# 64 tokens of block 2 gathered instead of 32 in a hybrid attention, mLSTM and PEER block

## The chip, the cores and the metric

The kernel runs on one core of one Trainium2 chip. The metric is the device time of one execution in microseconds; the number to compare is the median of several executions. The profile and its rows come from one further execution, with the hardware profiler on.

## The reference

One decoder layer over 512 tokens (and 16 meta tokens) of width 2048, all in float32. A mixer of differential attention and mLSTM comes first; its result is added to the residual stream. Then comes the part that this case is about, PEER, a layer of 16,384 small experts, of which each token takes 128:

```python
q = (ht @ w_q).reshape(T, PEER_HEADS, 2, PEER_SUB_DIM)
s = jnp.einsum('thpd,hpnd->thpn', q, sub_keys)
...
best_s, best_pos = lax.top_k(cand_s, PEER_TOPK)
idx = jnp.take_along_axis(cand_i, best_pos, axis=-1).reshape(T, PEER_HEADS * PEER_TOPK)
gate = jax.nn.softmax(best_s, axis=-1).reshape(T, PEER_HEADS * PEER_TOPK)
...
ub = jnp.take(u, ib, axis=0)
act = jax.nn.gelu(jnp.einsum('td,tkd->tk', hb, ub), approximate=False)
return jnp.einsum('tk,tkd->td', gb * act, jnp.take(v, ib, axis=0))
```

u and v are tables of 16,384 rows of 2048 floats (128 MB each). The residual is added and the result normalised.

## The kernel before

The tokens of PEER are four blocks of 128. The kernel treats them in two ways.

**Dense.** For the first ND = 352 tokens (blocks 0, 1 and 96 tokens of block 2) it computes all 16,384 experts. The table u is streamed in 128 chunks (`u_chunk`): a chunk of 128 experts is a 128 x 2048 slab, loaded in two halves of 512 KB from SP's queue, each split into a high and a low part (`split_half`: ACT casts hi, VectorE computes lo), and multiplied in 3 x 16 = 48 matmuls of ND columns (`mm3`, three products for float32 accuracy). ACT takes the gelu and stores the chunk of activations to `Ad`. The high and low parts have five buffers of half a chunk, the raw loads three.

Which expert a token takes is a one-hot matter: `ebuild` makes, for four tokens at a time, one-hot rows (`e`, `eg` on VectorE, `ea` on ACT, in bf16), `gbuild` multiplies them in 12 small matmuls (`pg`) into the gate matrix of these four tokens over all experts, and every 32 tokens (`TG`) a 2 MB store on SP's queue puts them in `Gd`. In the second half (V), the product of activation and gate is made per chunk (`p_mul` on VectorE, `p_split`: an ACT cast ah and a VectorE subtraction al) and the table v is streamed in 240 steps, each a half of 512 KB and 24 matmuls of ND columns (`tmm`, `py`), with `yadd` after each group, and a last group of 16 steps that transposes the result (`seed`, `vmm`).

**Gathered.** The other tokens, block 3 (128 tokens) and the last NB = 32 tokens of block 2, have their rows fetched. One gather step (`gather`, then `work`) is an indirect DMA from GpSimd that brings 128 rows of 8 KB, one for each partition, into one of three buffers `ug`, and one VectorE operation over 128 x 2048: a dot product with the token (rows of u, L844), or a weighted addition (rows of v, L857). Block 3 needs 128 steps for u and 128 for v. The NB tokens of block 2 are spread over the partitions in NQ = 128/NB groups of slots, so that they need SB = 128/NQ steps each way. `run(n)` carries the steps out up to the n-th of NJ and keeps three gathers ahead.

**Order.** PE's and VectorE's instructions are issued in the order written. In a chunk of U that is: the two VectorE splits of the next chunk, then the one-hots, then the gather steps that `pace` calls for; a gather is issued when the step three before it has left its buffer. `pace` spreads the steps up to the JU-th over the chunks from the first with one-hots to the end of U; V spreads the rest over its steps. The last UTAIL = 6 chunks of U stand in the V block, where they alternate with V's first preparations (`pro`).

Of the kernel before, what the change touches and what calls it, by code (L numbers as in the profile page):

```python
# [10 lines left out]
BF = mybir.dt.bfloat16  # L11
U32 = mybir.dt.uint32
I32 = mybir.dt.int32
AF = mybir.ActivationFunctionType
OP = mybir.AluOpType
# [14 lines left out]
NK = 128  # L30
# [5 lines left out]
UTAIL = 6  # L36
# [1 line left out]
VLL = 6  # L38
GLAG = 8
QPRE = 24  # L40
NB = 32
NQ = 128 // NB
SB = 128 // NQ
ND = S - 128 - NB
GROUPS = [8] + [16] * 7 + [8]
NJ = 2 * (128 + SB)
JU = 150
AR = 20
AR1 = 8

# [1 line left out]
def bcast(ap, n):  # L52
    return bass.AP(tensor=ap.tensor, offset=ap.offset, ap=[list(a) for a in ap.ap] + [[0, n]])


def bcast_mid(ap, n):
    a = [list(p) for p in ap.ap]
    return bass.AP(tensor=ap.tensor, offset=ap.offset, ap=a[:1] + [[0, n]] + a[1:])
# [607 lines left out]
def rest(tc, I, out, L):  # L666
    nc = tc.nc
# [18 lines left out]
    with tc.tile_pool(name="op", bufs=1) as op_, tc.tile_pool(name="pso", bufs=6, space=PSUM) as pso:  # L686
# [34 lines left out]
        for i, (p, pr) in enumerate(seq):  # L721
# [13 lines left out]
            for j in range(2):  # L735
                n = 2 * pr + j
# [6 lines left out]
            if p == 4 and pr in (2, 5):  # L743
                b = stores.pop(0)
# [41 lines left out]

    hB = dp.tile([NB, D], F, name="hB")
    hn = []
    for b in range(2):
        cs = slice(1024 * b, 1024 * b + 1024)  # L790
        t = wp.tile([128, 8, 128], F, name="nfr", tag="raw", bufs=3).rearrange("p a b -> p (a b)")
        src = I["nfr"][0:1, cs]
        nc.sync.dma_start(t, bass.AP(tensor=src.tensor, offset=src.offset, ap=[[0, 128], [1, 1024]]))
        t2 = wp.tile([128, 8, 128], F, name="hB", tag="raw", bufs=3).rearrange("p a b -> p (a b)")
        nc.vector.tensor_tensor(t2[128 - NB:], x1n[128 - NB:, 2, cs], t[128 - NB:], op=OP.mult)
        nc.scalar.dma_start(hB[:, cs], t2[128 - NB:])
        nc.vector.tensor_tensor(t, x1n[:, 3, cs], t, op=OP.mult)
# [19 lines left out]
    up = sU.enter_context(tc.tile_pool(name="up", bufs=1))  # L817
    iota = up.tile([128, 128], F, name="iota")
    nc.scalar.dma_start(iota, I["c_iota"])
    iota4 = up.tile([128, 128, 4], BF, name="iota4")  # L820
    nc.vector.tensor_copy(iota4, bcast(iota, 4))
    n1T = up.tile([128, ND], BF, name="n1T")
    n2T = up.tile([128, ND], BF, name="n2T")
    gp = up.tile([128, 3, ND], BF, name="gp")
    g0 = up.tile([128, ND], F, name="g0")
# [6 lines left out]
    def gather(j):  # L832
        kind, k = jobs[j]
        t = rows[j] = gr.tile([128, D], F, name="ug", tag="ug", bufs=3)
        ix = idx if kind in "da" else idxB
        nc.gpsimd.indirect_dma_start(out=t, out_offset=None, in_=I["un" if kind in "dD" else "vn"],  # L836
                                     in_offset=bass.IndirectOffsetOnAxis(ap=ix[:, k:k + 1], axis=0))
# [21 lines left out]
    def run(n, ready=NJ):  # L859
        while nj[1] < min(n, ready):  # L860
            while nj[0] < min(ready, nj[1] + 3):
                gather(nj[0])
                nj[0] += 1
            work(nj[1])
            nj[1] += 1
        while nj[0] < min(ready, nj[1] + 3):
            gather(nj[0])
            nj[0] += 1
# [23 lines left out]
    with tc.tile_pool(name="tk", bufs=1) as tk, \  # L892
# [142 lines left out]
        for q in range(NQ):  # L1035
            ps_, cs = slice(NB * q, NB * q + NB), slice(SB * q, SB * q + SB)
            nc.vector.tensor_copy(idxB[ps_], ids[128 - NB:, 2, cs])
# [8 lines left out]
        for src, dst in ((n1s, n1T), (n2s, n2T), (gs, None)):  # L1046
            pt = ptr.tile([128, ND], F, name="ptt", tag="ptt")
            for b in range(3):
                n = min(128, ND - 128 * b)
# [14 lines left out]
    with tc.tile_pool(name="gk", bufs=1, reuse_waits="tile") as gk, \  # L1064
            tc.tile_pool(name="psg", bufs=2, space=PSUM) as psg, \
            tc.manual_schedule(engines={mybir.EngineType.Pool}):
        stg = {}

        ge = {}

        def ebuild(q):
            t0 = 4 * q
            e = gk.tile([128, 2, 128, 4], BF, name="e", tag="e", bufs=2)
            eg = gk.tile([128, 2, 128, 4], BF, name="eg", tag="eg", bufs=2)
            ea = gk.tile([128, 4, 128], BF, name="ea", tag="ea", bufs=2)
            nc.vector.tensor_tensor(e[:, 0], iota4, bcast_mid(n1T[:, t0:t0 + 4], 128), op=OP.is_equal)
            nc.vector.tensor_tensor(e[:, 1], iota4, bcast_mid(n2T[:, t0:t0 + 4], 128), op=OP.is_equal)
            for i in range(2):
                nc.vector.tensor_tensor(eg[:, i], e[:, 1], bcast_mid(gp[:, 1 + i, t0:t0 + 4], 128), op=OP.mult)
            for j in range(4):  # L1080
                nc.scalar.activation(ea[:, j, :], e[:, 1, :, j], AF.Copy, scale=g0[:, t0 + j:t0 + j + 1])
            ge[q] = e[:, 0], [ea.rearrange("p j n -> p n j"), eg[:, 0], eg[:, 1]]

        def gbuild(q):
            tg, r = divmod(4 * q, TG)
            if r == 0:
                stg[tg] = gk.tile([128, NK, TG], F, name="stg", tag="stg")
            e1, eg = ge.pop(q)
            pg = psg.tile([128, 4, 128], F, name="pg", tag="pg")
            for j in range(4):  # L1090
                for i in range(3):
                    nc.tensor.matmul(pg[:, j, :], e1[:, :, j], eg[i][:, :, j], start=(i == 0), stop=(i == 2))  # L1092
            nc.scalar.copy(stg[tg][:, :, r:r + 4], pg.rearrange("p j n -> p n j"))
            if r + 4 == TG:
                nc.sync.dma_start(Gd[tg, :, 0:NK, :], stg[tg])

        gr2.append(sG.enter_context(tc.tile_pool(name="gr2", bufs=1, side="right")))
        acc["D"] = gr2[0].tile([128, D], F, name="h2nB", tag="h2nB")
        for q in range(NQ):
            nc.scalar.dma_start(acc["D"][NB * q:NB * q + NB], hB)  # L1100
        ng, n0, c0 = 0, nj[1], ci
        ebuild(0)

        def pace(c):
            run(n0 + int((c + 1 - c0) * (JU - n0) / (NK - c0)))

        for c in range(ci, NK - UTAIL):
            u_chunk(c)
            while ng < min(ND // 4, (c + 1 - ci) * (ND // 4) / (NK - 12 - ci)):
                gbuild(ng)  # L1110
                ng += 1
                if ng < ND // 4:
                    ebuild(ng)
            pace(c)
    sU.close()

    with ExitStack() as sV:
# [46 lines left out]
        def vsplit(i):  # L1164
            if i < len(vord):
                vs[i] = split_half(None, "v", vraw.pop(i))
# [6 lines left out]
        free, t0 = [], 0  # L1173
        for g in range(NG - 1):
            n = GROUPS[g]
            free += [t0 + n + 2 * (j // 2) + 2 for j in range(n)]
            t0 += 2 * n
        for q in range(GROUPS[0], NK):
            g = max(x for x in range(NG) if g0s[x] <= q)
            m, n = q - g0s[g], GROUPS[g - 1]  # L1180
            base = 2 * g0s[g - 1]
            t = base + (2 * n * m) // GROUPS[g]
            t = max(t, free[q - AR] if q >= AR else 0, base - 4)
# [9 lines left out]
        for c in range(NK - UTAIL, NK):  # L1193
            if c == NK - 1:
                for i in range(VLA):
                    vload(i)
                    vsplit(i)
            u_chunk(c)
            for _ in range(-(-len(pro) // (NK - c))):
                f, q = pro.pop(0)  # L1200
                f(q)
            pace(c)
        assert not pro
        sQ.close()
        sD.close()
# [111 lines left out]
        for i, (g, hf, pr, c) in enumerate(vord[:last]):  # L1317
# [9 lines left out]
            if i == nlast - 8:  # L1327
                for b in range(2):
                    t = wp.tile([128, 8, 128], F, name="nlw", tag="raw", bufs=3)
# [134 lines left out]
```

## Time and profile before

| what | before |
|---|---|
| median of 3 runs (lowest to highest) | 3327.83 us (3327.72 to 3330.03) |
| the profiled execution | 3331.74 us |
| its span, first to last instruction | 3330.0 us |
| mean granted TensorE clock | 0.992 of full speed |
| matmul busy (PE) | 3264.0 us, 98% |
| VectorE busy (DVE) | 2320.2 us, 70% |
| ScalarE busy (ACT) | 1325.5 us, 40% |
| GpSimd busy (POOL) | 943.9 us, 28% |
| moved by DMA | 815.47 MB, 245 GB/s over the span |

Busy times of one engine are unions of its instructions' spans; instructions of one engine may overlap slightly. PE is the matmul, PEld the weight load that goes beside it. The DMA share of a stretch is the time that packets took, over 16 DMA engines and the stretch. Lines (L844) are those of the kernel before.

### The profile page before, as it was taken

To read this page: it belongs to the slowest core of one execution; us is meant where nothing else is said; L and a number is where in the kernel's file an instruction comes from. 1 tells how busy PE (TensorE), PEld (TensorE's weight loads), DVE (VectorE), ACT (ScalarE), POOL (GpSimd) and SP (SyncE) were. 2 spreads that over 40 slices of the span, in tenths; PEclk is the share of its full clock that TensorE was granted. 3 is DMA by queue.
4 is the path that set the end of the run, shared out by engine and by line. 5 is a ranking of instruction groups with operands and counts; after the bars stand their busy time and mean duration, and the time that the engine had idled before them with its cause. 6 is when DMAs were issued, how large, how long until landed. Compare 5 with 4: busy or idle time off the path is not lost.

```text
span 3330.0 us, 51020 instructions
## 1 busy us (share of the span) xinstructions
PE 3264.0 (98%) x20126; PEld 3067.1 (92%) x20126; DVE 2320.2 (70%) x3504; ACT 1325.5 (40%) x2219; POOL 943.9 (28%) x942
## 2 busy tenths in 40 slices
PE   8999999999999999999999999997999999999998
PEld 7889898888887899999999999997999999999996
DVE  7444444444367788787877778767888888888973
ACT  5444444453252233444544544433333333333323
POOL 2011111110015566423332233322323323323312
PEclk8999999999999999999999999998999999999999
DMA  4222121123353266588888978999999999999972
GB/s 154 70 70 77 64 77 64 64 70 115 127 186 136 87 221 226 206 323 316 332 343 325 361 297 348 354 362 337 377 354 375 372 365 370 375 364 372 379 279 101
DMA packets 230162, 815.47 MB, mean 245 GB/s; under 512 B 21697, under 2 KB 85697, under 8 KB 186529
## 3 DMA queue, kind: packets, MB, share of 16 engines
q1 hardware_dynamic: 105488, 400.72, 33.3%
q0 software_dynamic: 46080, 335.56, 25.7%
q10 hardware_dynamic: 78352, 75.92, 6.8%
q8 instruction: 158, 2.59, 0.3%
q14 instruction: 84, 0.68, 0.1%
HBM read 757.33 MB, written 54.79 MB: 244 GB/s over the span
## 4 chain that ended last, share of the span: by engine, by line
PE 85%; DVE 8%; DMA 2%; issue 2%; ACT 1%; POOL 1%; ACTq 0%; SPq 0%; POOLq 0%; DVEq 0%
PE pu L89 10%; PE pu L90 10%; PE pu L91 10%; PE py L1275 8%; PE py L1277 8%; PE py L1276 8%; PE ps L89 5%; PE ps L91 5%; PE ps L90 5%; PE pg L1092 3%; PE po L742 2%; PE po L740 2%; PE po L741 2%; DVE y L857 1%; DVE lov L80 1%
## 5 line engine op out<-in xcount | busy, mean ns | idle before, releaser
L89 PE MATMUL pu<-hh,hid 128*128 128x352 f32 (+1 forms) x2272 | 759.8, 334 | 0.2 <-ACT at L889 0.2
L90 PE MATMUL pu<-hh,lod 128*128 128x352 f32 (+1 forms) x2272 | 751.3, 331 | 3.1 <-DVE lod L80 3.1
L91 PE MATMUL pu<-hl,hid 128*128 128x352 f32 (+1 forms) x2272 | 750.2, 330 | 0.0
L1275 PE MATMUL py<-ah,hiv 128*128 128x352 f32 x1920 | 627.0, 327 | 20.5 <-ACT hiv L79 9.5
L1276 PE MATMUL py<-ah,lov 128*128 128x352 f32 x1920 | 623.4, 325 | 8.8 <-DVE lov L80 8.8
L1277 PE MATMUL py<-al,hiv 128*128 128x352 f32 x1920 | 625.5, 326 | 0.0
L79 ACT CAST hiv<-rawv 128x1024 fp32r<-128x1024 f32 x256 | 269.2, 1053 | 572.4 <-PE py L1277 462.6
L80 DVE TENSOR_TENSOR lod<-rawd,hid 128x1024 fp32r<-128x1024 f32 x284 | 361.0, 1287 | 176.7 <-ACT hid L79 175.5
L90 PEld LDWEIGHTS pu<-hh,lod 128*128 128x128 f32 x2272 | 428.2, 188 | 12.8 <-DVE lod L80 3.4
L89 PEld LDWEIGHTS pu<-hh,hid 128*128 128x128 f32 x2272 | 429.9, 189 | 10.3 <-ACT at L889 0.8
L91 PEld LDWEIGHTS pu<-hl,hid 128*128 128x128 f32 x2272 | 428.1, 188 | 9.7
L79 ACT CAST hid<-rawd 128x1024 fp32r<-128x1024 f32 x284 | 297.8, 1050 | 347.2 <-DMA rawd<-in_u_dram 235.1
L89 PE MATMUL ps<-xh,hiz 128*128 128x256 f32 (+2 forms) x1280 | 410.9, 321 | 1.3 <-DVE qT L369 1.2
L836 POOL DMA_INDIRECT ug<-in_un_dram,idx x128 | 249.2, 1947 | 522.3 <-DVE ug L844 500.8
L91 PE MATMUL ps<-xl,hiz 128*128 128x256 f32 (+2 forms) x1280 | 392.8, 307 | 0.0
L90 PE MATMUL ps<-xh,loz 128*128 128x256 f32 (+2 forms) x1280 | 392.5, 307 | 0.0
L1275 PEld LDWEIGHTS py<-ah,hiv 128*128 128x128 f32 x1920 | 363.0, 189 | 24.2 <-issue 12.9
L1276 PEld LDWEIGHTS py<-ah,lov 128*128 128x128 f32 x1920 | 362.6, 189 | 11.8 <-DVE lov L80 11.8
L836 POOL DMA_INDIRECT ug<-in_vn_dram,idx x128 | 229.0, 1789 | 469.7 <-DVE y L857 444.3
L1277 PEld LDWEIGHTS py<-al,hiv 128*128 128x128 f32 x1920 | 361.9, 188 | 0.0
L80 DVE TENSOR_TENSOR lov<-rawv,hiv 128x1024 fp32r<-128x1024 f32 x256 | 313.4, 1237 | 33.7 <-ACT hiv L79 33.5
L857 DVE SCALAR_TENSOR_TENSOR y<-ug,act,y 128x2048 f32<-128x2048 f32 x127 | 298.3, 2349 | 14.8 <-DMA ug<-in_vn_dram,idx 14.8
(342 smaller groups left out, 5029.9 us busy)
## 6 DMA issues: line engine op xcount, KB each, us to landing
rawd<-in_u_dram SPq DMA_DIRECT2D x256, 512.0 KB
rawv<-in_v_dram SPq DMA_DIRECT2D x256, 512.0 KB
rawz<-in_wz_dram SPq DMA_DIRECT2D x98, 512.0 KB
Ad<-at ACTq DMA_DIRECT2D x128, 176.0 KB
Gd<-stg SPq DMA_DIRECT2D x11, 2048.0 KB
gt<-Gd ACTq DMA_DIRECT2D x32, 704.0 KB
av<-Ad ACTq DMA_DIRECT2D x64, 352.0 KB
rawwo<-in_wo_dram SPq DMA_DIRECT2D x40, 512.0 KB
```

The costliest lines, as they stand in the source:

```text
L79: nc.scalar.copy(hi, raw)
L80: eng.tensor_tensor(lo, raw, hi.bitcast(F), op=OP.subtract)
L89: nc.tensor.matmul(ps, a, xh[k][:, cs], start=(k == 0), stop=False)
L90: nc.tensor.matmul(ps, b, xh[k][:, cs], start=False, stop=False)
L91: nc.tensor.matmul(ps, a, xl[k][:, cs], start=False, stop=(k == KD - 1))
L740: nc.tensor.matmul(ps[tb], mh[n][:, sl], h, start=(n == 0), stop=False)
L836: nc.gpsimd.indirect_dma_start(out=t, out_offset=None, in_=I["un" if kind in "dD" else "vn"], in_offset=bass.IndirectOffsetOnAxis(ap=ix[:, ...
L857: nc.vector.scalar_tensor_tensor(acc[kind], t, o, acc[kind], op0=OP.mult, op1=OP.add)
L1092: nc.tensor.matmul(pg[:, j, :], e1[:, :, j], eg[i][:, :, j], start=(i == 0), stop=(i == 2))
L1275: nc.tensor.matmul(po, h, ah, start=(pr + j == 0), stop=False)
L1276: nc.tensor.matmul(po, l, ah, start=False, stop=False)
L1277: nc.tensor.matmul(po, h, al, start=False, stop=(2 * pr + j == n - 1))
```

## The change

Sixty-four tokens of block 2 are gathered instead of 32. With NB = 64 there are two groups of slots instead of four, SB is 64 instead of 32, the dense part has ND = 320 tokens instead of 352, and there are NJ = 384 gather steps instead of 320. JU, the number of them in U, goes from 150 to 208. `pace` now ends before the last six chunks of U, which call it no more. The one-hots lie in pairs of tokens instead of fours, so that neighbouring elements of one token are two bf16 apart instead of four.

```diff
-NB = 32
+NB = 64
 NQ = 128 // NB
 SB = 128 // NQ
 ND = S - 128 - NB
 GROUPS = [8] + [16] * 7 + [8]
 NJ = 2 * (128 + SB)
-JU = 150
+JU = 208
...
-    iota4 = up.tile([128, 128, 4], BF, name="iota4")
-    nc.vector.tensor_copy(iota4, bcast(iota, 4))
+    iota2 = up.tile([128, 2, 128, 2], BF, name="iota2")
+    for i in range(2):
+        nc.vector.tensor_copy(iota2[:, i], bcast(iota, 2))
...
+        def pairs(t):
+            a = [list(p) for p in t.ap]
+            return bass.AP(tensor=t.tensor, offset=t.offset, ap=[a[0], [2 * a[1][0], 2], [0, 128], [a[1][0], 2]])
+
         def ebuild(q):
             t0 = 4 * q
-            e = gk.tile([128, 2, 128, 4], BF, name="e", tag="e", bufs=2)
-            eg = gk.tile([128, 2, 128, 4], BF, name="eg", tag="eg", bufs=2)
-            ea = gk.tile([128, 4, 128], BF, name="ea", tag="ea", bufs=2)
-            nc.vector.tensor_tensor(e[:, 0], iota4, bcast_mid(n1T[:, t0:t0 + 4], 128), op=OP.is_equal)
-            nc.vector.tensor_tensor(e[:, 1], iota4, bcast_mid(n2T[:, t0:t0 + 4], 128), op=OP.is_equal)
+            e = gk.tile([128, 2, 2, 128, 2], BF, name="e", tag="e", bufs=2)
+            eg = gk.tile([128, 2, 2, 128, 2], BF, name="eg", tag="eg", bufs=2)
+            ea = gk.tile([128, 2, 2, 128], BF, name="ea", tag="ea", bufs=2)
+            nc.vector.tensor_tensor(e[:, 0], iota2, pairs(n1T[:, t0:t0 + 4]), op=OP.is_equal)
+            nc.vector.tensor_tensor(e[:, 1], iota2, pairs(n2T[:, t0:t0 + 4]), op=OP.is_equal)
             for i in range(2):
-                nc.vector.tensor_tensor(eg[:, i], e[:, 1], bcast_mid(gp[:, 1 + i, t0:t0 + 4], 128), op=OP.mult)
+                nc.vector.tensor_tensor(eg[:, i], e[:, 1], pairs(gp[:, 1 + i, t0:t0 + 4]), op=OP.mult)
             for j in range(4):
-                nc.scalar.activation(ea[:, j, :], e[:, 1, :, j], AF.Copy, scale=g0[:, t0 + j:t0 + j + 1])
-            ge[q] = e[:, 0], [ea.rearrange("p j n -> p n j"), eg[:, 0], eg[:, 1]]
+                nc.scalar.activation(ea[:, j // 2, j % 2, :], e[:, 1, j // 2, :, j % 2], AF.Copy,
+                                     scale=g0[:, t0 + j:t0 + j + 1])
+            ge[q] = e[:, 0], [ea.rearrange("p a b n -> p a n b"), eg[:, 0], eg[:, 1]]
...
                 for i in range(3):
-                    nc.tensor.matmul(pg[:, j, :], e1[:, :, j], eg[i][:, :, j], start=(i == 0), stop=(i == 2))
+                    nc.tensor.matmul(pg[:, j, :], e1[:, j // 2, :, j % 2], eg[i][:, j // 2, :, j % 2],
+                                     start=(i == 0), stop=(i == 2))
...
         def pace(c):
-            run(n0 + int((c + 1 - c0) * (JU - n0) / (NK - c0)))
+            run(n0 + int((c + 1 - c0) * (JU - n0) / (NK - UTAIL - c0)))
...
             for _ in range(-(-len(pro) // (NK - c))):
                 f, q = pro.pop(0)
                 f(q)
-            pace(c)
```

## Rows read from the trace of the kernel before

**Rows 1.** The page: busy time of PE, and GB/s in 40 slices.

```profile
PE 3264.0 (98%) x20126; PEld 3067.1 (92%) x20126; DVE 2320.2 (70%) x3504; ACT 1325.5 (40%) x2219; POOL 943.9 (28%) x942
...
GB/s 154 70 70 77 64 77 64 64 70 115 127 186 136 87 221 226 206 323 316 332 343 325 361 297 348 354 362 337 377 354 375 372 365 370 375 364 372 379 279 101
```

**Rows 2.** Busy by stage: length; PE, PEld, DVE, ACT, POOL; clock; DMA share; GB/s.

```profile
1165.00:1420.00 255.00, 255.00 (x1582) 254.84 (x1581) 206.47 (x500) 95.73 (x144) 139.12 (x215) 1.00 0.61 215
1420.00:2217.00 797.00, 796.43 (x5370) 784.39 (x5368) 617.16 (x783) 376.45 (x707) 248.78 (x126) 1.00 0.88 337
2217.00:2264.00 47.00, 41.74 (x246) 40.63 (x244) 33.75 (x40) 17.33 (x26) 14.49 (x7) 0.96 0.89 334
2264.00:2400.00 136.00, 119.93 (x686) 116.65 (x687) 102.31 (x107) 47.38 (x72) 40.22 (x24) 0.94 0.95 357
2400.00:3185.00 785.00, 773.72 (x4761) 770.58 (x4760) 687.85 (x640) 252.44 (x295) 255.37 (x143) 1.00 0.97 368
```

**Rows 3.** PE in order of time, 352 and 256 columns: start, length in us.

```profile
1503.11 0.32 PE L90 MATMUL pu<-hh,lod 128*128 128x352 f32 x1
1503.27 0.32 PE L91 MATMUL pu<-hl,hid 128*128 128x352 f32 x1
...
251.32 0.28 PE L90 MATMUL ps<-xh,loz 128*128 128x256 f32 x1
...
252.15 0.28 PE L91 MATMUL ps<-xl,hiz 128*128 128x256 f32 x1
```

**Rows 4.** The chain that ended last, two builds that follow one another in U.

```profile
1519.67 1.20 PE pg L1092 x12
...
1528.55 1.21 PE pg L1092 x12
```

**Rows 5.** DVE in order of time, from a one-hot build through two gather steps.

```profile
1520.91 0.43 DVE L1076 TENSOR_TENSOR e<-iota,n1T 128x512 bf16<-128x512 bf16 x1 [0.56 <-PE pg L1092]
...
1522.38 2.28 DVE L844 SCALAR_TENSOR_TENSOR ug<-ug,h2n 128x2048 f32<-128x2048 f32 x1
...
1524.59 2.29 DVE L844 SCALAR_TENSOR_TENSOR ug<-ug,h2n 128x2048 f32<-128x2048 f32 x1
```

**Rows 6.** DVE in V (2400 to 3185): groups by line, and its main wait.

```profile
L857 DVE SCALAR_TENSOR_TENSOR y<-ug,act,y 128x2048 f32<-128x2048 f32 x120 | 281.8, 2349 | 14.8 <-DMA ug<-in_vn_dram,idx 14.8
...
L1146 DVE TENSOR_TENSOR al<-tm,ah 128x352 fp32r<-128x352 f32 x97 | 51.0, 526 | 72.0 <-ACT ah L1145 72.0
L1135 DVE TENSOR_TENSOR tm<-av,gt 128x352 f32<-128x352 f32 x97 | 50.5, 521 | 0.0
...
L1287 DVE TENSOR_TENSOR yT<-yT,py 128x352 f32<-128x352 f32 x104 | 48.3, 519 | 7.0 <-PE py L1277 7.0
```

**Rows 7.** Gather issues (L836) by stage: POOL's busy time and count.

```profile
953.00:1420.00 467.00, 29.51 (x18) 1.00 0.50 172
1420.00:2217.00 797.00, 248.78 (x126) 1.00 0.88 337
2217.00:2264.00 47.00, 14.49 (x7) 0.96 0.89 334
```

**Rows 8.** Busy by stretch, as rows 2, of three stretches with the DMA full.

```profile
3120.00:3170.00 50.00, 50.00 (x309) 50.00 (x308) 42.39 (x33) 14.77 (x16) 18.79 (x10) 1.00 1.00 401
2820.00:2920.00 100.00, 98.10 (x606) 97.58 (x605) 88.47 (x83) 31.79 (x38) 32.77 (x19) 1.00 1.00 381
2020.00:2040.00 20.00, 20.00 (x140) 19.59 (x139) 15.20 (x19) 8.22 (x16) 6.61 (x4) 1.00 1.02 417
```

**Rows 9.** Waits in main U (1420 to 2217): total us, times, longest.

```profile
ACT hid L79 <- DMA rawd<-in_u_dram: 224.3, 106, 9.0
...
ACT stg L1093 <- DMA Gd<-stg: 32.0, 9, 6.2
```

**Rows 10.** DVE operations in bf16, groups by line over the whole span.

```profile
L1079 DVE TENSOR_TENSOR eg<-e,gp 128x512 bf16<-128x512 bf16 x176 | 67.0, 422 | 3.0
...
L967 DVE TENSOR_TENSOR eqb<-iom,bpb 128x800 bf16<-128x800 bf16 x32 | 18.4, 575 | 1.1
```

## The prediction

> **What bounds the kernel now.** The page comes first: PE is busy 98% of a span of 3330.0 us, and the DMA rate climbs from some 70 GB/s early to 340 to 380 in the second half [rows 1]. A mean over 3330 us says nothing on a change in two stages, so the second view is busy time by stage [rows 2]. The five rows are the first 32 U chunks (1165 to 1420), the 90 U chunks with one-hots and gathers (1420 to 2217, "main U"), the last six U chunks (to 2264), the start of V, and steady V (2400 to 3185). In all but the third and fourth PE is busy nearly throughout: 255 of 255, 796 of 797, 774 of 785. What the reader is to see is the columns beside it. In main U the DMA share is already 0.88 at 337 GB/s and in V 0.97 at 368; DVE is busy 617 of 797 and 688 of 785. PE ends last now, but DMA and DVE stand right behind it.
>
> Main U holds 5370 matmuls, that is 90 chunks of 48 and some 88 builds of 12; chunk and build together take 8.88 us, from one build in the chain to the next [rows 4], of which the build is 1.20. V's 4761 matmuls at 24 a step are 198.4 steps, 785/198.4 = 3.957 us each.
>
> **The change part by part.**
>
> *Narrower matmuls.* A 352-column matmul starts 0.16 us after the one before; the first and the last of eight of 256 columns start at 251.32 and 252.15, 0.1186 apart each [rows 3]. Between them a column costs (0.160 - 0.1186)/96 = 0.43 ns, so 320 columns should start every 0.146 us: 14 ns less, 0.67 us less in a chunk of 48 and 0.34 in a V step of 24. A line through two widths that enclose the new one excludes that nothing is gained. If PE stayed the bound everywhere, this is 128 x 0.67 + 240 x 0.34 = 167 us, and eight builds fewer save 10 more.
>
> *Early U, 32 chunks.* PE is busy all the time, DVE 206 of 255 and DMA at 0.61 [rows 2]. Gathers stay as they were (18 issued by then [rows 7], 15 of them used, since three run ahead). 32 x 0.67 = -21 us; DVE would then be busy 206 of 234, which still covers it. Bounds: 0 if the routing work on DVE takes over, -22 in full.
>
> *Main U, the gathers.* Before, 126 gathers are issued here [rows 7]. The new pace reaches 208 at the last of 90 chunks: 208 - 15 = 193 steps, 67 more, 2.14 a chunk where it was 1.4. Each is 128 rows of 8 KB, 1.049 MB. Three resources then have to be summed:
> - PE: 4320 x 0.146 = 631, and 80 builds of 1.20 = 96: 727 us.
> - DVE: a gather step occupies it from 1522.38 to 1524.59, 2.21 us, and a one-hot build from 1520.91 to 1522.38, 1.47 us [rows 5]. 617 + 67 x 2.21 - 8 x 1.47 = 753 us.
> - DMA: 337 GB/s x 797 us = 268.6 MB. Plus 67 x 1.049 = 70.3, less one 2.1 MB store of Gd and 90 x 16 KB of Ad (1.5 MB): 335.3 MB. What rate can be held is nowhere shown directly, since nothing ever held it for 800 us; the nearest rows with a share of 1.00 or over are 381 GB/s for 100 us, 401 for 50 us and 417 for 20 us [rows 8]. That gives 880, 836 and 804 us. I take the middle of the two longer ones, 391 GB/s: 857 us, 9.5 us a chunk.
>
> So main U ceases to be PE's and becomes DMA's: 857 - 797 = +60 us, with bounds +7 (417 held) and, if the in-order queues lose another half microsecond a chunk, +103 (10.0 us a chunk).
>
> [...]
>
> *What is queued behind a late gather.* DVE runs in written order: the two splits of the next chunk (lod), the four one-hot operations, then two gather steps. If a row is not there, the next chunk's lod stands behind it and PE runs dry a chunk later. Today what is late in main U is u itself, 224 us of ACT waiting for rawd, hidden by the look-ahead of five halves, and 32 us of ACT waiting for the Gd store, which shares SP's queue with u [rows 9]. With a saturated DMA this cover goes.
>
> *U's last six chunks.* They lose their gather steps (the removed pace call; seven were issued there before [rows 7]) and get 6 x 48 x 0.146 = 42 us of PE instead of 47: -4. The V prologue's loads move nowhere.
>
> *V.* PE falls to 24 x 0.148 = 3.55 us a step. But DVE was nearly as full as PE: 688 us busy, and 72 us in which it stands between tm and al because ACT must cast ah first [rows 6]. That wait is part of the order written down, so DVE is occupied 760/198.4 = 3.83 us a step. After: 176 steps of gathers in 237 V steps instead of some 170, +0.026 x 2.35 = +0.06 us; tm, al and yT shrink by at most an eleventh of some 0.5 us each, -0.05 to -0.07. DVE's floor stays at 3.83. DMA: 368 x 3.957 = 1.456 MB a step, +0.027 for gathers, -0.02 for Gd and Ad: 1.463 MB, 3.84 us at 381 GB/s and 3.65 at 401. V can therefore gain from 0 (gather waits take it back) to 0.127 us a step; I take half, 3.89 us: 240 x 0.067 = -16 us, bounds 0 and -30. PE's 0.34 us a step is lost to DVE.
>
> *One-hots in pairs.* No row shows the pair layout. Four of these DVE operations cost 422 ns each at 512 elements; eqb (bf16, 575 ns for 800 elements) scales to 368, tm (fp32, 521 ns for 352) to 758 [rows 6, 10]. 80 builds x 4 x (758 - 422) = +107 us of DVE at worst, which would fill main U's 857 to 860; at best -17. The operands keep their type and the same element count, so I take the row of fours, 422, and nothing on the path. On PE the build can only get cheaper than 1.20 us, and PE isn't main U's end any more: 0. The remaining edits (half as many copies of idxB, wB and fold, two loads of hB instead of four of the same bytes, 64-row seeds) are each a few operations of a microsecond or less: 0.
>
> *Sum.* -21 + 60 - 4 - 16 = +19 us. The profiled execution took 3331.74 us (3330.0 of span and 1.7 around it), 3.9 above the median of the runs. 3331.7 + 19 - 3.9 = 3347 us. A measurement of this kernel can tell some 0.2%, 6.7 us, from no change.
>
> **The rivals.**
> - *DMA carries more (faster).* Place: main U. Mechanism: packets that follow one another without pause move faster than the mixed windows show, so that 410 GB/s is held: 335.3/0.410 = 818, +21; V then reaches DVE's floor, -30. -21 + 21 - 5 - 30 = -35: 3293 us. For it: 417 GB/s over 20 us, at full share [rows 8]. Against: over 100 us it is 381. It decides from 400 GB/s held: there main U is +41 and the sum 0. [...] Chance 0.33.
> - *The queues trip over each other (much slower).* Late gathers on DVE, the 2 MB Gd store ahead of u on SP's queue and PE pauses that lower its granted clock (it is 0.94 in the start of V, where PE is busy 120 of 136 [rows 2]) add up to 10 us a chunk, and V gains nothing: -21 + 103 - 4 = +78: 3406 us. For: the waits of [rows 9] exist already. Against: five halves and three gather buffers of look-ahead. Chance 0.14.
> - *PE stays the bound, the change does all that it can:* 3328 - 177 = 3151 us. Against: main U at 727 us would need 461 GB/s, above every row. Chance 0.03.
>
> **How the numbers follow.** The forecast, main U bound by DMA between 381 and 401 GB/s, has 0.50, and its own range is 3325 to 3370: 0.41 of the 0.50 lie above 3334.5, 0.08 within 0.2% and 0.01 below. Of the first rival 0.27 is faster and 0.06, its upper end, within 0.2%. The second is slower, the third faster. Faster: 0.27 + 0.03 + 0.01 = 0.31. Same: 0.08 + 0.06 = 0.14. Slower: 0.41 + 0.14 = 0.55. The 8-in-10 range runs from 3285, which leaves out the third rival (0.03) and the lowest fifth of the first (0.06), to 3402, which leaves out the upper half of the second (0.07).
>
> **What would show it.** Right: matmuls of 320 columns 0.146 us apart while PE does not wait; main U longer, not shorter, than 797 us, at a DMA share near 1.0 and 385 to 400 GB/s; PE busy about 85% there; DVE rows that wait for ug from in_un_dram; early U about 21 us shorter; V steps near 3.89 us with PE waiting for lov. Wrong: a main U that stays under 830 us (rate above 404 GB/s), a V step under 3.83 us (DVE's order costs less than I count), or one-hot operations far from 422 ns.

## The result, and the profile after

The changed kernel takes 3371.84 us (median of 4 runs, 3367.35 to 3374.81), the kernel before 3327.77 beside it on the same chip: a ratio of 1.013, 95% interval 1.0114 to 1.0146, slower by 44 us. The forecast had 3347, that is +19. The profiled execution took 3374.45 us with a span of 3372.7, 42.7 more than before. First the page: busy time of PE, its granted clock in tenths and GB/s in 40 slices, which answer [rows 1].

```profile
PE 3134.0 (93%) x20026; PEld 2914.4 (86%) x20030; DVE 2423.0 (72%) x3565; ACT 1299.2 (39%) x2175; POOL 1056.6 (31%) x1006
...
PEclk9999999999999999998999988989999999999999
...
GB/s 152 75 69 76 63 72 69 73 64 119 140 206 92 118 249 248 274 372 368 359 371 381 363 364 363 380 397 319 371 372 379 366 367 380 366 377 381 349 355 111
```

PE went from 98% to 93% busy, so in part of the span the kernel now waits for something else. Where the time went shows in the busy times by stage of the changed kernel, with the columns of [rows 2]: early U, main U, U's last six chunks, V's first 40 steps, its next 180, and V as a whole.

```profile
1167.00:1393.00 226.00, 226.00 (x1547) 225.19 (x1546) 187.81 (x493) 88.73 (x137) 150.96 (x211) 1.00 0.72 237
1393.00:2282.00 889.00, 756.77 (x5252) 730.21 (x5252) 744.52 (x865) 357.77 (x666) 352.25 (x190) 0.92 0.96 371
2282.00:2330.00 48.00, 41.89 (x271) 41.52 (x269) 29.09 (x33) 17.48 (x26) 3.76 (x4) 0.93 0.87 316
2330.00:2492.00 162.00, 147.99 (x965) 144.47 (x964) 133.95 (x124) 60.34 (x85) 50.19 (x29) 0.98 0.97 364
2492.00:3210.00 718.00, 662.45 (x4316) 654.28 (x4315) 626.67 (x585) 227.56 (x270) 238.79 (x135) 0.96 0.97 369
...
2330.00:3281.00 951.00, 881.39 (x5761) 869.47 (x5760) 821.06 (x763) 309.90 (x379) 308.12 (x173) 0.97 0.97 369
```

[rows 2] cut the stages a little differently, so these are the same stages of the kernel before, cut at the same instructions: early U, V's first 40 steps, its next 180, and V as a whole.

```profile
1170.00:1420.00 250.00, 250.00 (x1549) 249.84 (x1548) 201.78 (x498) 92.47 (x140) 136.18 (x211) 1.00 0.62 217
...
2264.00:2445.00 181.00, 164.93 (x964) 161.65 (x964) 141.79 (x146) 61.83 (x90) 54.38 (x31) 0.95 0.96 359
2445.00:3158.00 713.00, 701.72 (x4316) 698.58 (x4316) 627.68 (x581) 230.14 (x270) 232.83 (x131) 1.00 0.98 370
2264.00:3237.00 973.00, 945.65 (x5765) 939.23 (x5766) 828.33 (x780) 315.07 (x384) 302.75 (x170) 0.99 0.96 363
```

So early U is -24 us, main U 889 - 797 = +92, the last six chunks +1, V -22, and what lies around them (1170 and 93 us before, 1167 and 92 after) -4: +43. One stage went wrong, main U, and it lost what all the others gained and as much again.

Main U's waits name who stood still. These are VectorE's waits and those of SP's queue in that stretch: engine, line, what for; us in total, times, longest.

```profile
DVE lod L80 <- ACT hid L79: 46.8, 31, 8.1
DVE ug L845 <- DMA ug<-in_un_dram,idx: 45.8, 27, 5.8
DVE ug L845 <- DMA ug<-in_un_dram,idxB: 32.9, 14, 4.9
DVE yB L858 <- DMA ug<-in_vn_dram,idxB: 11.2, 5, 6.2
...
SPq L72 <- DVE lod L80: 576.3, 100, 13.1
```

VectorE is busy 745 of the 889 us and stands 46.8 + 45.8 + 32.9 + 11.2 = 137 us for data: together 882. That the busy time and the waits of one engine fill its stage proves nothing by itself; they did so before too, when PE was the end. What changed is what VectorE waits for. These are its waits in main U of the kernel before:

```profile
DVE lod L80 <- ACT hid L79: 113.2, 52, 8.9
DVE e L1076 <- PE pg L1092: 61.3, 35, 7.3
DVE ug L844 <- DMA ug<-in_un_dram,idx: 1.3, 1, 1.3
```

It stood 61 us for PE and hardly ever for a gathered row; now it stands 90 us for rows and some 3 for PE. Late u was there before and is not new.

The SP row suggests a ring. SP can issue the next half of u only when VectorE's split (lod) has given a raw buffer back (576 us of waiting, where the kernel before had 535 in a stage 92 us shorter; part of this is only SP running ahead, so the sum shows no loss), so a VectorE that waits for a gathered row can also hold back the load of u that it will need next, and then wait for that. This is VectorE's timeline just after the 2 MB store of Gd at 1540.0 us; brackets are idle time and what ended it.

```profile
1547.11 1.23 DVE L80 TENSOR_TENSOR lod<-rawd,hid 128x1024 fp32r<-128x1024 f32 x1 [1.88 <-ACT hid L79]
...
1555.02 2.29 DVE L845 SCALAR_TENSOR_TENSOR ug<-ug,h2n 128x2048 f32<-128x2048 f32 x1 [3.01 <-DMA ug<-in_un_dram,idx]
...
1558.05 1.23 DVE L80 TENSOR_TENSOR lod<-rawd,hid 128x1024 fp32r<-128x1024 f32 x1 [0.73 <-ACT hid L79]
1561.76 1.23 DVE L80 TENSOR_TENSOR lod<-rawd,hid 128x1024 fp32r<-128x1024 f32 x1 [2.49 <-ACT hid L79]
```

A split waits 1.9 us for u, a gather step 3.0 us for its row, the next two splits 0.7 and 2.5 us for u again. SP's load of u at 1559.30 us goes out as the split of 1558.05 ends, so the buffer does come back by that way. But the halves that the splits of 1558.05 and 1561.76 waited for had, by the count of three buffers, been issued at 1540.40 and 1545.25, before the wait for the row. The rows show late u and late rows in turn; that one makes the other late is argued, not shown.

The smaller promises held. PE in order of time, across the end of a chunk and a one-hot build (start, length):

```profile
1497.02 0.31 PE L90 MATMUL pu<-hh,lod 128*128 128x320 f32 x1
1497.17 0.31 PE L91 MATMUL pu<-hl,hid 128*128 128x320 f32 x1
1497.32 0.23 PE L1098 MATMUL pg<-ea,e 128*128 128x128 bf16 x1
...
1497.98 0.39 PE L89 MATMUL pu<-hh,hid 128*128 128x320 f32 x1
```

Matmuls of 320 columns start 0.15 us apart, as worked out, and a build takes 1497.98 - 1497.32 = 0.66 us instead of the 1.20 of [rows 4]. VectorE's one-hot operations keep their 422 ns (groups by line):

```profile
L1084 DVE TENSOR_TENSOR eg<-e,gp 128x512 bf16<-128x512 bf16 x160 | 60.9, 422 | 2.7
```

### The profile page after: what moved, and what is told of

The parts are those of the page before. It is cut to its first block, busy times and chain, and to the rows that moved or that the text cites. A ratio compares the mean times of both kernels' runs of the same rounds, so it can differ in the third digit from the quotient of the medians.

```text
span 3372.7 us, 50871 instructions
## 1 busy us (share of the span) xinstructions
PE 3134.0 (93%) x20026; PEld 2914.4 (86%) x20030; DVE 2423.0 (72%) x3565; ACT 1299.2 (39%) x2175; POOL 1056.6 (31%) x1006
## 3 DMA queue, kind: packets, MB, share of 16 engines
q1 hardware_dynamic: 105344, 398.62, 32.9%
## 4 chain that ended last, share of the span: by engine, by line
PE 48%; issue 20%; DVE 11%; POOL 10%; DMA 8%; ACT 2%; POOLq 0%; ACTq 0%; SPq 0%; DVEq 0%
POOL ug L837 9%; PE ps L89 5%; PE ps L91 5%; PE ps L90 5%; PE py L1282 4%; PE py L1281 4%; PE py L1283 4%; PE pu L90 3%; PE pu L91 3%; PE pu L89 3%; DVE y L858 3%; DMA ug<-in_vn_dram,idxB 2%; DVE lov L80 2%; DVE yB L858 2%; DMA rawv<-in_v_dram 2%
## 5 line engine op out<-in xcount | busy, mean ns | idle before, releaser
L90 PE MATMUL pu<-hh,lod 128*128 128x320 f32 (+1 forms) x2272 | 751.7, 331 | 96.8 <-DVE lod L80 95.7
L89 PE MATMUL pu<-hh,hid 128*128 128x320 f32 (+1 forms) x2272 | 748.1, 329 | 34.5 <-ACT hid L79 31.5
L91 PE MATMUL pu<-hl,hid 128*128 128x320 f32 (+1 forms) x2272 | 740.2, 326 | 0.0
L1282 PE MATMUL py<-ah,lov 128*128 128x320 f32 x1920 | 607.3, 316 | 42.9 <-DVE lov L80 42.5
L1281 PE MATMUL py<-ah,hiv 128*128 128x320 f32 x1920 | 604.9, 315 | 26.7 <-DVE yT L1293 26.1
L1283 PE MATMUL py<-al,hiv 128*128 128x320 f32 x1920 | 603.4, 314 | 0.0
L90 PEld LDWEIGHTS pu<-hh,lod 128*128 128x128 f32 x2272 | 446.1, 196 | 120.7 <-DVE lod L80 111.4
L89 PEld LDWEIGHTS pu<-hh,hid 128*128 128x128 f32 x2272 | 445.9, 196 | 46.3 <-ACT hid L79 33.3
L91 PEld LDWEIGHTS pu<-hl,hid 128*128 128x128 f32 x2272 | 447.5, 197 | 9.7
L845 DVE SCALAR_TENSOR_TENSOR ug<-ug,h2n 128x2048 f32<-128x2048 f32 x128 | 290.0, 2286 | 45.8 <-DMA ug<-in_un_dram,idx 45.8
```

What stands on the lines that cost most here:

```text
L89: nc.tensor.matmul(ps, a, xh[k][:, cs], start=(k == 0), stop=False)
L90: nc.tensor.matmul(ps, b, xh[k][:, cs], start=False, stop=False)
L91: nc.tensor.matmul(ps, a, xl[k][:, cs], start=False, stop=(k == KD - 1))
L845: nc.vector.scalar_tensor_tensor(t, t, 1.0, acc[kind], op0=OP.mult, op1=OP.mult, accum_out=o)
L1281: nc.tensor.matmul(po, h, ah, start=(pr + j == 0), stop=False)
L1282: nc.tensor.matmul(po, l, ah, start=False, stop=False)
```

## The experiments

Theory 1 at the start was that main U is bound by its bytes alone, at a rate lower than I had taken. Theory 2 was that DMA and VectorE are both nearly full and, working in a written order, stop each other. Times of single runs stand without an interval; "before" had a median of 3325.8 to 3330.9 us beside all of them. The same kernel's runs differ by up to 16 us (four_bufs and gd_act below), so a stage difference of some 15 us in one profile proves little.

**half_dve and half_bytes: relieve one side at a time.** Half of each dot product and weighted sum, or half of each row's bytes.

```diff
# half_dve, in work()
+            h = slice(0, D // 2)
-            nc.vector.scalar_tensor_tensor(t, t, 1.0, acc[kind], ...)
+            nc.vector.scalar_tensor_tensor(t[:, h], t[:, h], 1.0, acc[kind][:, h], ...)
# half_bytes, in gather(); work() then reads that half twice
-        nc.gpsimd.indirect_dma_start(out=t, out_offset=None, in_=I["un" ...],
+        nc.gpsimd.indirect_dma_start(out=t[:, :D // 2], out_offset=None,
+                                     in_=I["un" ...].rearrange("n (a d) -> (n a) d", a=2),
...
```

> The changed kernel with full gathers, but each VectorE operation of a gather step goes over 1024 columns instead of 2048 (half of each dot product and half of each sum are left out): VectorE has some 1.07 us less per step, 206 us in main U. Theory 1 (the DMA holds 371 GB/s in this mix and no more, main U is bytes over rate): main U stays within 875 to 895, V gains nothing, 3355 to 3372 us. Theory 2 (the DMA could hold 391, but VectorE's in-order work of 753 us and the late gathers take turns in stopping each other): main U falls to 845 to 860 and V to 3.75 us a step, 3290 to 3320 us.

> The changed kernel, but each gather brings 128 rows of 4 KB instead of 8 KB, and VectorE goes over the half that came twice, so that its work stays what it was; the result is that of other rows. If the DMA sets main U (either theory of how), 193 steps there bring 101 MB less, DMA needs under 640 us, and main U falls from 889 to VectorE's floor of 753, say 760 to 785; V falls to VectorE's 3.83 us a step, some -30. In all 3372 - 110 - 30, about 3230 us. If PE with its lowered clock or VectorE set main U, it stays above 850.

Measured: 3269.21 us and 3265.91 us. Main U by windows, first of half_dve, then of half_bytes:

```profile
1394.00:2235.00 841.00, 734.77 (x5281) 715.64 (x5278) 555.01 (x870) 352.54 (x670) 250.07 (x193) 0.94 1.00 398
```

```profile
1391.00:2192.00 801.00, 729.97 (x5246) 707.62 (x5244) 740.12 (x865) 360.12 (x666) 415.66 (x190) 0.96 0.82 289
```

With VectorE relieved, the same bytes move at 398 GB/s and a share of 1.00, over 841 us. So DMA can carry what the forecast took (391) and a little more, and theory 1 falls: 889 us is not DMA's own limit. With DMA relieved to a share of 0.82, main U still needs 801 us, of which VectorE is busy 740. Neither side alone gives 889; both together do. Of the two, theory 2 stands, though neither run came out in the range given for it: half_dve was faster (841 and 3269, not 845 to 860 and 3290 to 3320), half_bytes slower (801 and 3266, not 760 to 785 and about 3230), since VectorE still stands 801 - 740 = 61 us there, at least 25.6 + 15.9 of them for rows. Nor does half_dve relieve VectorE alone: GpSimd takes 250/193 = 1.3 us for issuing a gather there, and 352/190 = 1.85 in the changed kernel.

**four_bufs: a fourth gather buffer in U.**

```diff
+        if gk4 and j < JU and (j - j4[0]) % 4 == 0:
+            t = rows[j] = gk4[0].tile([128, D], F, name="ug4", tag="ug4")
+        else:
             t = rows[j] = gr.tile([128, D], F, name="ug", tag="ug", bufs=3)
...
-            while nj[0] < min(ready, nj[1] + 3):
+            while nj[0] < min(ready, nj[1] + (4 if gk4 else 3)):
```

> The changed kernel with a fourth gather buffer, and four gathers ahead, in main U alone. Theory 1 (bytes over a fixed rate): main U stays within 1% of 889, 3360 to 3375 us. Theory 2 (three buffers let VectorE and DMA stop each other): main U gains 15 to 40 us, 3330 to 3357 us.

Measured: 3365.89 us, ratio 1.0108 (1.0092 to 1.0124); main U 879 us (1394 to 2273). The time lies in theory 1's range and the gain of ten microseconds is under theory 2's. VectorE's waits in main U say why:

```profile
DVE lod L80 <- ACT hid L79: 115.5, 54, 12.3
...
DVE ug L848 <- DMA ug<-in_un_dram,idx: 2.9, 1, 2.9
DVE yB L861 <- DMA ug<-in_vn_dram,idxB: 2.9, 1, 2.9
```

The waits for rows fell from 90 to 7 us, and the wait for u rose from 47 to 116. The lateness did not go; it passed from the rows to u, where three raw buffers do not cover it. GpSimd took 381/191 = 2.0 us an issue here, so a slow issue by itself does not make rows late.

**raw5: five raw buffers for u instead of three, in main U.** An alternate pool holds two of every five.

```diff
-            raw = (rawp or wp).tile([128, 8, 128], F, name="raw" + name, tag="raw", bufs=3)
+            nl[0] += 1
+            if xp and nl[0] % 5 in (1, 3):
+                raw = xp[0].tile([128, 8, 128], F, name="rawx" + name, tag="rawx", bufs=2)
+            else:
+                raw = (rawp or wp).tile([128, 8, 128], F, name="raw" + name, tag="raw", bufs=3)
...
```

> Five buffers instead of three for the raw halves of u in the 90 chunks. Theory 'late u': ScalarE's 417 us of waiting for u reach PE through VectorE's split (lod), so two halves more of look-ahead shorten the 90 chunks to 850-870 us, time 3335-3355. Rival 'late gathers': VectorE is stopped by its own rows, which more u in flight makes later still: 885-900 us, time 3366-3385.

Measured: 3348.74 us (3348.66 to 3352.62), ratio 1.0062 (1.0045 to 1.0078); this interval lies wholly below that of the changed kernel. Main U by windows, and VectorE's waits in it:

```profile
1396.00:2253.00 857.00, 743.37 (x5252) 721.20 (x5252) 743.28 (x865) 353.62 (x667) 353.31 (x190) 0.93 0.98 382
```

```profile
DVE ug L850 <- DMA ug<-in_un_dram,idx: 59.2, 36, 6.9
DVE ug L850 <- DMA ug<-in_un_dram,idxB: 34.3, 20, 5.2
DVE yB L863 <- DMA ug<-in_vn_dram,idxB: 13.5, 8, 4.7
DVE yB L861 <- DMA ug<-in_vn_dram,idxB: 3.5, 1, 3.5
DVE lod L85 <- ACT hid L84: 1.4, 1, 1.4
```

The split's wait for u fell from 46.8 to 1.4 us, the DMA share rose to 0.98, and main U is 857 us, the figure of the forecast. VectorE: 743 busy and 59.2 + 34.3 + 13.5 + 3.5 + 1.4 = 112 waiting. The rival, "more u under way makes the gathers later", has a small part in it: waits for rows rose from 90 to 110 us. Five raw buffers and a fourth gather buffer together were not run.

**gd_act, smooth, smooth_act, raw5_gd_act: the store of Gd.** In the changed kernel 85 of the 137 us that VectorE waits for data in main U lie within 25 us after one of the ten 2 MB stores, so the store was moved to ScalarE's queue (gd_act, and raw5_gd_act with five raw buffers), or cut into eight behind the builds, on SP's queue (smooth) or on ScalarE's (smooth_act); these two keep one staging tile throughout.

```diff
# gd_act, raw5_gd_act
-                nc.sync.dma_start(Gd[tg, :, 0:NK, :], stg[tg])
+                nc.scalar.dma_start(Gd[tg, :, 0:NK, :], stg[tg])
# smooth (smooth_act: nc.scalar), at every build
...
-            if r + 4 == TG:
-                nc.sync.dma_start(Gd[tg, :, 0:NK, :], stg[tg])
+            z = NK // (TG // 4) * (r // 4)
+            nc.sync.dma_start(Gd[tg, :, z:z + NK // (TG // 4), :], stg[tg][:, z:z + NK // (TG // 4), :])
```

> The changed kernel with the 2 MB stores of Gd issued from ACT's queue instead of SP's, where the loads of u stand behind them. In the changed kernel some 84 of 120 us of VectorE's longer waits in main U lie within 25 us after one of the ten stores. Theory A (order in SP's queue: u waits behind the store, and with it VectorE and then the gathers): main U falls from 889 by 25 to 50 us, 3320 to 3347 us in all. Theory B (the burst takes 5 us of every DMA engine whatever its queue): main U stays within 10 us, 3360 to 3375 us.

> Each 2 MB store of Gd becomes eight stores of 256 KB, one behind each build, of the same total bytes (each stores an eighth of the rows of the staging tile as they stand then, so most of the stored numbers are incomplete; time only). Theory 'bursts': the ten stores set off the stops of VectorE in the 90 chunks, so without them this stage shrinks from 889 to 845-865 us and the time is 3325-3350. Rival 'chain of waits': any late transfer stops VectorE, whichever transfer it is behind, and bytes are unchanged: 880-892 us and 3360-3378.

> The eight small stores of Gd behind each build again (most of the stored numbers are incomplete; time only), but issued on ScalarE's queue, so that no load of u stands behind a store that waits for its build. If the loss of the run before came from SP's order, it is gone: 90 chunks at 892 us or less instead of 969. If the 2 MB bursts themselves cost the changed kernel time, the 90 chunks fall to 845-870 us and the time to 3330-3350; if bursts cost nothing by themselves: 880-892 us, time 3362-3375.

> Five raw buffers and the 2 MB stores on ScalarE's queue. Theory 'look-ahead of u': what matters is how many halves of u are under way, and with five of them a load that SP holds back behind a store is covered: no further change, 90 chunks 850-860 us, time 3343-3355. Rival 'SP order on top': the ten held-back loads still cost, 835-848 us, time 3325-3342.

Measured: gd_act 3371.23 us, ratio 1.0134 (1.0117 to 1.0151), no gain, as theory B had it; smooth 3450.59, 1.0367 (1.0345 to 1.0389); smooth_act 3363.98, main U 875; raw5_gd_act 3360.27, 1.0099 (1.0081 to 1.0117), worse than raw5 and outside both its ranges. Smooth failed both its theories, and its waits say why (main U, 1393 to 2363; SP's queue, then VectorE):

```profile
SPq L1105 <- ACT ea L1086: 539.5, 66, 12.9
...
DVE lod L80 <- ACT hid L79: 155.6, 62, 10.4
```

The small store comes in every chunk, and SP's queue stands 540 us ahead of it for the build that ScalarE has not finished; every load of u behind it loses its look-ahead, and VectorE's wait for u trebles, from 47 to 156 us. Moved to ScalarE's queue the same stores give 875 us. That is 14 less than the changed kernel, between the two theories and within what one run can show: whether the bursts cost anything by themselves stays open, and if so, it is not the main part. Moving the ten big stores to ScalarE's queue gains nothing that can be told (gd_act) or costs 12 us (raw5_gd_act). What their place on SP's queue costs is not isolated by that: in gd_act's profile, its fastest run, VectorE's wait for u fell from 47 to 26 us, but its waits for rows rose from 90 to 106 and ScalarE's for the store from 40 to 63 (1393 to 2280 in both).

**fours: the changed kernel with one-hots in fours,** that is, `ebuild`, `gbuild` and the iota of the kernel before.

> The changed kernel with its one-hots in fours as before. Forecast's step 'pairs 0': PE is not the end of the 90 chunks now, so a build of 1.20 instead of 0.66 us costs nothing much: 889-896 us there, time 3368-3380. Rival: PE's share comes back in full, as it did in the old kernel (21 us): 905-915 us there, time 3388-3398.

Measured: 3379.53 us, ratio 1.0152 (1.0135 to 1.0169), an interval that overlaps that of the change. Main U:

```profile
1395.00:2282.00 887.00, 780.00 (x5259) 758.74 (x5257) 746.50 (x866) 359.97 (x665) 348.46 (x190) 0.93 0.96 374
```

PE is busy 23 us more and the stage is not longer. Here pairs are worth nothing that can be told.

**pairs_alone, pairs_gd_act, pairs_raw5, pairs_raw5_ju166: the same edits on the kernel before.** One-hots in pairs on it; then with the store on ScalarE's queue; with five raw buffers; and with those and 166 instead of 150 gather steps in U.

```diff
# pairs_raw5_ju166, on top of pairs_raw5
-JU = 150
+JU = 166
```

> The kernel before with the one-hots in pairs and nothing else. In the changed kernel's trace a build of 12 matmuls takes 0.66 us where it took 1.20. With PE the bound of main U as before, 88 x 0.54 = -47 us, and the 268.6 MB then move at 358 GB/s, under the 371 seen: about 3283 us (3278 to 3295). If the DMA or VectorE stands in the way already at 358 GB/s, less: 3300 or more.

> The kernel before with the one-hots in pairs, and the Gd stores on ACT's queue. Pairs alone gave 3306 us with main U at 772 us, 22 above the 750 that PE's shorter builds allow. Theory A: these 22 us come from u behind the store, main U falls to 752 to 762, 3285 to 3296 us. Theory B: no change, 3300 to 3310 us.

> The old kernel with one-hots in pairs and five raw buffers for u in the 90 chunks. There PE was busy 762 of 772 us and DMA at 0.91, so look-ahead has little left to give: 750-765 us, time 3288-3300. Rival: late u is hidden there, no change, 3303-3309.

> The old kernel with pairs, five raw buffers and 166 instead of 150 gather steps in U. PE had 750 of 752 us in the 90 chunks with DMA at 0.92, so 16 more gathers (17 MB, 285 MB in all, 379 GB/s over 752 us) should nearly fit under it, as the forecast's floors say: 90 chunks 752-770 us, V 971 to 945-962 (PE is busy 943 there), time 3262-3280. Rival: near a full DMA the waits lengthen the 90 chunks by 2 us a gather or more, as in the changed kernel: 785 us or more there and 3285-3305.

Measured: 3305.83 us, ratio 0.994 (0.9927 to 0.9954); 3340.34, 1.004 (1.0026 to 1.0054); 3287.18, 0.9892 (0.987 to 0.9914); 3275.36, 0.9826 (0.981 to 0.9843). Main U of pairs_alone and of pairs_raw5, and main U and V of the last:

```profile
1417.00:2189.00 772.00, 761.30 (x5375) 748.78 (x5372) 614.59 (x783) 368.13 (x707) 246.66 (x126) 1.00 0.91 348
```

```profile
1416.00:2169.00 753.00, 750.11 (x5323) 739.16 (x5324) 619.29 (x783) 368.45 (x709) 244.81 (x126) 1.00 0.92 355
```

```profile
1420.00:2177.00 757.00, 753.87 (x5351) 742.40 (x5351) 647.62 (x813) 367.46 (x706) 283.91 (x141) 1.00 0.96 372
2225.00:3181.00 956.00, 938.64 (x5760) 935.50 (x5761) 794.26 (x748) 316.01 (x383) 273.67 (x154) 0.99 0.93 352
```

Where PE is the end, the pairs gain: 88 builds x (1.20 - 0.66) = 48 us are offered, 797 - 772 = 25 taken, while VectorE's split waits 143 us for u. Five raw buffers cut that wait to 44 and give another 19. PE is then busy 750 of 753 us. The 16 further gathers cost main U 4 us and free 15 in V. The store on ScalarE's queue costs pairs_alone 35 us, outside both theories, and the changed kernel nothing; why isn't settled: ScalarE's wait for the store grew from 39.7 to 93.7 us and VectorE's for u from 143 to 194, but no run takes this apart.

**width_alone, ju180, ju224: what the added gathers cost, and where.** The changed kernel without the 64 added steps (32 in U and in V each, and JU 150), and with other splits between U and V.

```diff
# width_alone; the lists of jobs are halved with it
-NJ = 2 * (128 + SB)
-JU = 208
+NJ = 2 * (128 + SB // 2)
+JU = 150
# ju180 (ju224: 224)
-JU = 208
+JU = 180
```

> The changed kernel without the 64 added gather steps (half of block 2's gathered tokens get no sums; 150 of 320 steps in U as before): the narrower matmuls and the pairs alone. Early U 226, main U at PE's or the DMA's floor (686 and some 265 MB at 371 to 398 GB/s, 666 to 714): 700 to 735 where it was 797. V at VectorE's 3.83 us a step or a little under, -15 to -30. 3327 - 24 - 80 - 22, about 3200 us (3180 to 3235). If it were 3150 or less, V would be PE's and VectorE's in-order waits would not count.

> The changed kernel with 180 of the 384 gather steps in U instead of 208 (its old share). If a step in main U costs what the trace of the changed kernel says, some 1.4 us of rate and 2.2 of VectorE with their waits, 28 fewer take 60 to 90 us from main U (800 to 830), and V, whose VectorE is full, pays 28 x 2.3 = 65 us: 3345 to 3372 us. If V had room (PE or DMA its bound), under 3330.

> 224 gather steps in U instead of 208. The step from 180 to 208 cost the U part 51 us and gave V 98. Theory 'straight line': V gives 3.5 us a gather again, U takes 1.8: V 951 to about 895-915, main U 889 to about 918, time 3340-3360. Rival 'knee': V's steps at 3.99 us are already near the floor of VectorE's order (width alone had 3.92 with 138 gathers in V), so V falls only to 935-948 and the time is 3378-3400.

Measured: 3236.84, 3423.22 and 3391.64 us. Main U of width_alone, then main U and V of ju180 and of ju224:

```profile
1391.00:2166.00 775.00, 719.30 (x5282) 706.97 (x5280) 623.07 (x768) 351.97 (x669) 273.33 (x135) 0.96 0.91 353
```

```profile
1395.00:2242.00 847.00, 742.88 (x5279) 717.74 (x5276) 688.68 (x826) 353.70 (x665) 317.07 (x165) 0.94 0.93 359
2281.00:3330.00 1049.00, 912.29 (x5761) 893.89 (x5762) 882.79 (x804) 307.94 (x379) 362.01 (x201) 0.94 0.96 362
```

```profile
1392.00:2343.00 951.00, 772.63 (x5252) 749.75 (x5250) 781.75 (x881) 359.24 (x665) 379.26 (x206) 0.89 0.95 365
2391.00:3299.00 908.00, 864.20 (x5766) 855.78 (x5767) 787.02 (x752) 310.98 (x381) 290.85 (x157) 0.98 0.98 368
```

Narrower matmuls and pairs alone gain 3326 - 3237 = 90 us, of which pairs_alone had 21 on the kernel before. But main U of width_alone was expected at 700 to 735 us and took 775, no less than the 772 of pairs_alone, with PE busy 719, VectorE 623 and DMA at 0.91: no engine fills it, and VectorE waits 148 us for u. So without one added gather this stage was already longer than any of its floors. The 64 gathers then cost 3372 - 3237 = 135 us, 2.1 us each, nearly the 2.2 us that a step occupies VectorE; 889 - 775 = 114 of them fall in main U.

Shifting them doesn't help. From 208 to 180 steps in U, main U gains 42 us and the last six chunks 9, and V loses 98 (3.5 us a step), more than the theory had given it, and ju180 missed its range. From 208 to 224, V gains 43 (2.7 a step) and main U loses 62 (3.9 a step). Either way from 208 the stage that takes steps loses more than the other gains, and neither has room. For ju224 neither theory came out whole: "straight line" had V right (908 us), but main U lost twice what it said; "knee" had the time right (3378 to 3400), but not V.

## Why the prediction was right on the sign and wrong on the size

Term by term, forecast and measured, in us: early U -21 and -24; main U +60 and +92; the last six chunks -4 and +1; V -16 and -22; the rest 0 and -4; sum +19 and +43.

**What held.** 320 columns 0.15 us apart, one-hot operations at 422 ns, "nothing on the path" for the pairs (fours), and VectorE's 753 us in main U (745). The bytes held too: 371 GB/s x 889 us = 330 MB, forecast 335.3. PE ceased to be main U's end and is busy 85% there, DVE rows that wait for ug are there, and PE waits 30 us for lov in V's steady steps. The rate of 385 to 400 GB/s in main U (371) and the V step of 3.89 us did not come.

**The step that failed** is "Three resources then have to be summed", with the longest taken as the stage: main U at DMA's 857 us. The term was +60 us and measured +92. The rate behind it was not the fault: half_dve held 398 GB/s with the same bytes, and by an estimate from main U's row DMA moved 371/0.96 = 386 GB/s while it was busy and stood idle for 0.04 x 889 = 36 us. The fault was to lay VectorE's 753 us beside DMA's 857 as if 104 us of slack lay between them, and to rest u on "the look-ahead of five halves". Five are the split buffers; of raw loads, the ones under way in the DMA, there are three, and SP issues a load when VectorE has freed one. The working itself says of that cover "With a saturated DMA this cover goes", and its sum gives that nothing; the price stands only in the bound of +103. What the runs showed in its place is an overlap that does not hold: VectorE stood 137 us for late u and late rows while DMA had idle time left, and width_alone's main U was over all its floors without the added gathers. Five raw buffers take the wait for u away and give 857 us and 3349, against 857 and 3347 in the forecast. That the numbers meet so closely is partly luck, since runs of one kernel scatter by several microseconds and the rate there was 382, not 391. What remains then, 110 us of VectorE waiting for rows, goes with a DMA share of 0.98, nearly full.

Two slips in the working change nothing: the first rival's sum takes -5 for the last six chunks where the part has -4, and V's matmul is put at 0.148 us without a working, where 0.146 was worked out.

**The rivals.** "DMA carries more" needed over 400 GB/s held; 398 was the most that any stage showed, and 371 what the changed kernel got. "The queues trip over each other" named the right mechanism, late gathers on VectorE and late u, and put main U at 900; it got 889. It was wrong on V, which it gave no gain, and two of its three parts are not shown to have a share: moving the store away from u on SP's queue gave nothing in all (gd_act), though it changed the waits, and the clock is unlikely to set the end. The granted clock in main U is 0.92 on average, before 1.00. Of its 889 windows of 1 us, 725 show it at 1.00 of full speed, 116 at 0.50 and the other 48 in between; by an estimate from the mean that is (1 - 0.92)/0.5 x 889 = 142 us at 0.50, in a stage in which PE waits 90 us for lod. But with the clock at 0.94, half_dve filled DMA to 1.00, and in the changed kernel VectorE's waits for PE come to about 3 us. No run holds the clock at 1.00 in this stage. I gave this rival 0.14; the rows [rows 9] spoke for more.

**V** came out at -22 against -16, and not in the way forecast. The steady steps got no shorter: 713 us for 180 of them before, 718 after, 3.99 us each and not 3.89. These are VectorE's groups in those 180 steps after the change:

```profile
L858 DVE SCALAR_TENSOR_TENSOR y<-ug,act,y 128x2048 f32<-128x2048 f32 x115 | 270.0, 2348 | 12.4 <-DMA ug<-in_vn_dram,idx 12.2
...
L1153 DVE TENSOR_TENSOR al<-tm,ah 128x320 fp32r<-128x320 f32 x91 | 44.8, 493 | 76.8 <-ACT ah L1152 76.8
...
L858 DVE SCALAR_TENSOR_TENSOR yB<-ug,wB,yB 128x2048 f32<-128x2048 f32 x19 | 44.6, 2349 | 2.6 <-DMA ug<-in_vn_dram,idxB 2.6
```

Busy 627, 77 between tm and al, 15 for rows: 718 of 718 us, and none for PE, while PE waits 30 us for lov and 26 for yT. So VectorE was most likely the end of the steady steps (before: 628 busy); relieving it brought V as a whole from 951 to 903 us (half_dve), relieving DMA to 934 (half_bytes). The forecast's floor of 3.83, a mean over a longer stretch, was 0.08 to 0.16 too low there. The gain lies at both ends: 19 us in the first 40 steps, and 79 - 71 = 8 after the 220th. Why those got shorter was not taken apart.

## What to carry to other kernels

Before taking a stage's longest floor for its time, ask whether the loads under way keep its engines from waiting. Here VectorE at 84% and DMA at 96% made a stage longer than either, with VectorE using two kinds of loads in a written order and freeing the buffers of both. A further buffer for one kind passed lateness on to the other: a fourth gather buffer (waits for rows from 90 to 7 us, for u from 47 to 116) gave ten microseconds of main U, two more raw buffers (for u from 47 to 1.4, for rows from 90 to 110) 32. Count look-ahead in the buffers that the DMA writes, not in those behind them. And part a change into its edits: here the pairs and two raw buffers alone took the old kernel to 3287 us, 0.989, and 16 gathers moved into U to 3275 us, 0.983 (0.981 to 0.9843), the best version found, while the 64 gathers for the 32 further tokens cost 135 us, and what they bought, the narrower matmuls, saved 90 together with the pairs.

## What the runs showed of the hardware

With the one-hots two bf16 elements apart instead of four, a build of 12 small matmuls takes 0.66 us, 55 ns each, instead of the 1.20, 100 ns each, of [rows 4]. Mixed traffic (loads of u, gathered rows of 8 KB, stores) held 398 GB/s for 841 us at a DMA share of 1.00 (half_dve, main U).
